# Strassen from the third column pair on, and spatial weights transposed between gate and up, in a two-layer hybrid trunk

## The chip, the cores and the metric

The kernel runs on one core of a Trainium2 chip. The metric is the device time in microseconds from one launch, median over runs. Four engines compute: TensorE (PE, with its weight loads PEld), VectorE (DVE), ScalarE (ACT) and GpSimd (POOL). SyncE (SP) issues transfers (DMAs); an engine's instructions, and a queue's, run in their order.

## The reference

Two layers, 512 tokens, width 1024, all float32. h is the residual stream.

```python
def swiglu(x, w_gu, w_down):
    gate, up = jnp.split(x @ w_gu, 2, axis=-1)
    return (jax.nn.silu(gate) * up) @ w_down

h = h + 0.5 * rmsnorm(swiglu(rmsnorm(h, norm_g[0]), ffn1_gu, ffn1_down), norm_g[1])
z = rmsnorm(h, norm_g[2]) @ w_in      # split into: HGRN2 recurrence, window attention, spatial gating
mixed = jnp.concatenate([o_a, o_b, o_c], axis=-1) @ w_out
h = h + rmsnorm(mixed, norm_g[3])
h = h + 0.5 * rmsnorm(swiglu(rmsnorm(h, norm_g[4]), ffn2_gu, ffn2_down), norm_g[5])
gate = jax.nn.sigmoid(rmsnorm(h, norm_g[6]) @ ple_gate)
h = h + rmsnorm((p_i @ ple_proj) * gate, norm_g[7])
```

The hidden width of the two feed-forward networks (FFN) is 2816, so each has a gate-up matrix of 1024 x 5632 and a down matrix of 2816 x 1024. The spatial gating uses a 128 x 128 lower-triangular matrix per group and layer, sgw; the kernel needs it transposed and masked.

## The kernel before

Every float32 product is made of three products of reduced-precision halves: a value is cast on ScalarE to its high half (L142, L296 and L334, "whi", "uwh") and the difference to the value is the low half, made on VectorE (L139, "wlo", "uwl"). TensorE then adds hi·hi, hi·lo and lo·hi in PSUM.

The phases are ffn1, mix, ffn2 and ple, twice. Each phase ends with a list of chains, one for each of four token tiles: the post-norm of the phase's result, the addition to h (L201) and the pre-norm of the next phase (hn, L225), then transposes on TensorE (ptr, L231) that give hT, the moving operand of the next phase. Of these tile 0 and 1 are transposed at the border, tile 2 and 3 inside the next phase.

An FFN has 11 column pairs, mp = 0 to 10: 256 gate columns and the same 256 up columns. Pair 0 is multiplied plainly, in two halves of the tokens, 192 matmuls of 256 columns (L254). Pairs 1 to 10 use Strassen's scheme on 2 x 2 blocks (halves of the contraction and of the tokens): seven products M1, M2, M5, M6, M3, M7, M4 of 24 matmuls each (L379), with sums of hT blocks made once (token_sums: S1 to S4) and sums of weight blocks made per pair (operands: four raw loads b11, b21, b12, b22 at L329 and five subtractions at L339). Results accumulate in three PSUM banks X, Y, Z. silu(gate)·up goes to a tile g, is stored to DRAM (gd, L416 for pair 0 and L458 for the others) and is loaded again as gl (L484) for the down projection (accs, L249 to L251). M4 of a pair is held back behind M1 of the next pair, except for the last pair.

The order: a scheduler places instructions by their dependences and priorities, except that those passed through pin (keep_in_program_order) keep the order of the program among themselves. Strassen's matmuls are pinned; pair 0's, the raw loads and the g stores are not. issue_after ("behind") puts instructions behind named ones. Weights are staged in two buffers "wst"; buffers "z" and "u" hold raw weights of odd and even pairs. The spatial weights are loaded, transposed (L650) and masked (L652) by mix_params, which a hook calls at k = 4 of the down projection. The stores of h ahead of mix are issued by SP in make_pre.

Of the kernel before, what the change touches and what calls it, by code (L numbers as in the profile page):

```python
# [20 lines left out]
P = 128  # L21
# [51 lines left out]
def kernel(ctx: ExitStack, tc: tile.TileContext, a: dict, out: bass.AP, phases=None):  # L73
# [52 lines left out]
    def tsl(t):  # L126
        return slice(t * P, (t + 1) * P)
# [151 lines left out]
    def ffn(l, w_gu, w_down, i, ends, hook):  # L279
# [4 lines left out]
        def four(x):  # L284
            return x[:].rearrange("p (a b) -> p a b", a=4)
# [5 lines left out]
        for gu in range(2):  # L291
            for q in range(2):
                st = wpool.tile([P, 1024], F32, tag="wst", name="wst", bufs=WST)
                nc.sync.dma_start(four(st), w_view(0, gu, q))
                hi, lo = first[q] if gu == 0 else w_pair()
                nc.scalar.copy(hi[:], st[:])  # L296
                split_lo(lo[:], st[:], hi[:], nc.gpsimd if gu == q == 0 and i == 0 else nc.vector)
                w[gu, q] = hi, lo
        yield
        yield  # L300
        hT = hTs[i]
        turn(0)
        turn(1)

        def token_sums():
            def whole(half, q, tag):
                x = ut("A32", "z") if tag == "z" else wpool.tile([P, 1024], F32, tag=tag, name="A32", bufs=WST)
                hi, lo = (hT[1][y][:, :, HALVES[half]].bitcast(F32) for y in (q, 2 + q))
                pin(nc.vector.tensor_tensor(out=four(x), in0=hi, in1=lo, op=ALU.add))
                return x  # L310

            def make(n, x, y, op, out):
                nc.vector.tensor_tensor(out=out[:], in0=x[:], in1=y[:], op=op)
                nc.scalar.copy(S[n][0][:], out[:])
                split_lo(S[n][1][:], out[:], S[n][0][:])

            a21, a22 = (whole(1, q, "wst") for q in range(2))
            make(1, a21, a22, ALU.add, a22)
            a11 = whole(0, 0, "z")
            make(3, a11, a21, ALU.subtract, a21)  # L320
            make(2, a22, a11, ALU.subtract, a11)
            a12 = whole(0, 1, "z")
            make(4, a12, a11, ALU.subtract, a12)


        def operands(mp):
            def raw(gu, q):
                x = ut("wraw", "z" if mp % 2 else "u")
                nc.sync.dma_start(four(x), w_view(mp, gu, q))  # L329
                return x  # L330

            def split(x):
                hi, lo = w_pair()
                nc.scalar.copy(hi[:], x[:])  # L334
                split_lo(lo[:], x[:], hi[:])
                return hi, lo

            def sub(out, x, y):
                nc.vector.tensor_tensor(out=out[:], in0=x[:], in1=y[:], op=ALU.subtract)  # L339
# [12 lines left out]
            yield split(b22)  # L352
            yield split(b12)
            yield split(b21)
# [14 lines left out]
        def pin(ins):  # L369
            return tc.keep_in_program_order(ins)  # L370
# [9 lines left out]
                                             stop=m == 1 and k == 3 and n == 2, skip_group_check=True))  # L380


        acc = {(m, gu): ps(f"gu{m}{gu}", ("pg", "pm")[m]) for m in range(2) for gu in range(2)}

        def stream():
            for mp in range(1, NMP):
                for (name, kind), w in zip(MS, operands(mp)):
                    yield mp, name, kind, w
        ahead, queue = stream(), []
# [4 lines left out]
                if x:  # L394
                    queue.append(x)

        prefetch(1)
        for tok in HALVES:
            for m in range(2):
                for gu in range(2):  # L400
                    mms = [(k, x) for x in range(3) for k in range(KD)]
                    for k, x in mms:
                        hi, lo = w[gu, k // 4]
                        c = slice((k % 4) * 256 + m * P, (k % 4) * 256 + m * P + P)
                        mm1(acc[m, gu][:, tok], (hi[:, c], lo[:, c]), hT_k(hT, k, tok), x, (k, x) == mms[0], (k, x) == mms[-1])
                    if tok.stop == 256 and 2 * m + gu in FT:
                        turn(2 + FT.index(2 * m + gu))
                if tok.stop == 512:
                    sg = ut("sg", "r")
                    nc.scalar.activation(sg[:], acc[m, 0][:], AF.Silu)  # L410
                    nc.vector.tensor_tensor(out=G[:, m * 512:(m + 1) * 512], in0=acc[m, 1][:], in1=sg[:], op=ALU.mult)
            if tok.stop == 256:
                G = wpool.tile([P, 1024], F32, tag="wst", name="g", bufs=WST)
                token_sums()
                prefetch(2)
        nc.sync.dma_start(gd[0][:], G[:])  # L416


        LOOK = 4
# [8 lines left out]
        def step(mp, name, kind, w):  # L428
# [17 lines left out]
                d["c12"] = ut("c12", "r")  # L446
                nc.scalar.copy(d["c12"][:], X[:])
            if name == "M3":
                d["G"] = wpool.tile([P, 1024], F32, tag="wst", name="g", bufs=WST)
                add(out=d["c12"][:], in0=Z[:], in1=d["c12"][:], op=ALU.add)  # L450
                add(out=g_half(d["G"], 0), in0=m2(d["c12"]), in1=m2(d["c11"]), op=ALU.mult)
            if name == "M7":
                add(out=d["c22"][:], in0=X[:], in1=d["c22"][:], op=ALU.add)  # L453
            if name == "M4":
                sg = ut("sg", "r")
                nc.scalar.activation(sg[:], X[:], AF.Silu)
                add(out=g_half(d["G"], 1), in0=m2(sg), in1=m2(d["c22"]), op=ALU.mult)
                nc.sync.dma_start(gd[mp][:], d["G"][:])  # L458

        held = None  # L460
        while True:
            prefetch(LOOK - len(queue))
            if not queue:
                break
            x = queue.pop(0)
            if x[1] == "M4" and x[0] < NMP - 1:
                held = x
                continue
            step(*x)
            if x[1] == "M1" and held:  # L470
                step(*held)
                held = None

        gpost, npre = ends()
        ORD = {0: "pt", 1: "pg", 2: "pm", 3: "pm"}
        accs = {(t, n): ps(f"acc{t}{n}", ORD[t]) for t in range(NT) for n in range(2)}
        ws, gs = {}, {}
        for k in range(KF):
            if k == 4:
                hook()  # L480
# [6 lines left out]
            gs[k] = tuple(x[:, (k % 2) * 512:(k % 2 + 1) * 512] for x in (gh, gl))  # L487
            if k < KF - TAIL:
                for t in range(NT):
                    for n in range(2):  # L490
                        mm3(accs[t, n][:], cut(gs[k], tsl(t)), ws[k](n * 512), k == 0, False)
# [9 lines left out]
    def ple(l, i, ends):  # L501
# [5 lines left out]
                              a["p"][l, 0, j * 256:(j + 1) * 256, :].rearrange("(t p) c -> p t c", p=P))  # L507
        pT = []
        for k in range(2):
            pt = ps("ppT", "pm")  # L510
# [12 lines left out]
        for t in range(NT):  # L523
# [10 lines left out]
            for u, (n, k) in enumerate(steps):  # L534
# [5 lines left out]
            ys = []  # L540
            for n in range(2):
                y = ut("y", "t")
                nc.scalar.activation(y[:], gt[n][:], AF.Sigmoid)
                out_ = y if t < NT - 1 else pj[n]
                nc.vector.tensor_tensor(out=out_[:], in0=pj[n][:], in1=y[:], op=ALU.mult)
                ys.append(out_[:])
# [3 lines left out]
        chains.append((NT - 1, ys, gpost, 1.0, npre))  # L550
        close_phase()


# [580 lines left out]
    def make_pre(i):  # L1134
# [26 lines left out]
    state = {"setup": not mixers}  # L1161

    def hook_for(i):
        def hook():
            if i + 1 < len(seq) and seq[i + 1][1] == "mix":
                if not state["setup"]:
                    mix_setup()
                    state["setup"] = True
                prms[i + 1] = mix_params(seq[i + 1][0])
        return hook  # L1170

    def phase(i):
# [9 lines left out]
            pass  # L1182

    if seq[0][1] == "mix":
        hook_for(-1)()
    def load_x(t):
        for n in range(2):
            nc.sync.dma_start(h[t][n][:], a["x"][0, tsl(t), HN[n]])
# [8 lines left out]
    next(run)  # L1197
    load_x(2)
    load_x(3)
    pre(2)  # L1200
    pre(3)
    for i in range(len(seq)):
        drain(run)
        todo = list(chains)
# [38 lines left out]
```

## Time and profile before

| what | value |
|---|---|
| median of three runs | 2054.29 us (2050.96, 2054.56, 2054.29) |
| profiled execution | 2056.59 us |
| its span, first to last instruction | 2054.8 us |
| mean granted TensorE clock | 0.985 |
| TensorE busy | 1969.0 us (96%) |
| VectorE, ScalarE busy | 1398.7 us (68%), 925.7 us (45%) |
| GpSimd busy | 113.2 us (6%) |
| instructions | 31098 |

A row of a group gives line, engine, operation, the names out<-in, then busy time and mean duration; a row of waits gives the waiting engine and line, the releaser, and the time in total, the times, and the longest. In rows of windows there follow, behind the window and its length, the busy time (and the count) of PE, PEld, DVE, ACT and POOL, the granted clock, the DMA share and GB/s. Rows of the chain and of the timeline start with the time in us since the first instruction and the duration.

### The profile page before, as it was taken

Reading aid. Unit: us, or ns where it says so; the run is one execution under the profiler, and the core shown is the slowest. Engines: PE = TensorE matmul, PEld = TensorE weight load, DVE = VectorE, ACT = ScalarE, POOL = GpSimd, SP = SyncE. Lnnn points to the kernel's source line nnn. Section 1 sums busy time; section 2 is a strip of 40 time slices with the busy share of each in tenths; the row PEclk is TensorE's granted clock in tenths of the full one; section 3 lists DMA queues with packets and bytes.
Section 4 is the critical chain, followed back from the end, with each engine's and each line's share of the span. In section 5 each row is a group of like instructions: output and inputs, shape, how many; then the busy total and the mean of one; then the engine's idle time right before and its main releaser. Section 6 shows DMA issues by size and latency. Waiting matters only on the chain.

```text
span 2054.8 us, 31098 instructions
## 1 busy us (share of the span) xinstructions
PE 1969.0 (96%) x12524; PEld 1765.8 (86%) x12524; DVE 1398.7 (68%) x2062; ACT 925.7 (45%) x1467; POOL 113.2 (6%) x135
## 2 busy tenths in 40 slices
PE   7899999899999999999989999998999999999998
PEld 6899978688678999888779999786887799998876
DVE  6887753669768888434688886436697688883364
ACT  4445443455444545333445444334555444453252
POOL 1000000112100000000100000001130000000000
PEclk9999999999999999999999999999999999999999
DMA  5434264323404434453234443543232153425431
GB/s 183 142 125 145 72 231 134 103 75 92 130 22 143 153 108 131 143 164 134 82 103 144 126 132 97 197 139 97 62 114 98 42 174 117 141 87 185 159 113 52
DMA packets 160034, 251.18 MB, mean 122 GB/s; under 512 B 11409, under 2 KB 116753, under 8 KB 159889
## 3 DMA queue, kind: packets, MB, share of 16 engines
q1 hardware_dynamic: 159888, 249.19, 37.9%
q8 instruction: 98, 1.61, 0.3%
q14 instruction: 48, 0.39, 0.1%
HBM read 217.17 MB, written 29.36 MB: 120 GB/s over the span
## 4 chain that ended last, share of the span: by engine, by line
PE 66%; DVE 8%; DMA 3%; ACT 2%; issue 1%; POOL 1%; SPq 0%; DVEq 0%; POOLq 0%; ACTq 0%
PE X L379 16%; PE Z L379 9%; PE acc L249 5%; PE acc L251 5%; PE acc L250 5%; PE Y L379 4%; PE gu L254 3%; DMA wraw<-in_ffn_gate_up_dram 1%; PE gate L251 1%; PE gate L249 1%; PE gate L250 1%; DMA wst<-in_ffn_down_dram 1%; PE wo L249 1%; PE ptr L231 1%; PE wo L251 1%
## 5 line engine op out<-in xcount | busy, mean ns | idle before, releaser
L334 ACT CAST whi<-wraw 128x1024 fp32r<-128x1024 f32 x280 | 292.1, 1049 | 371.7 <-DVE wraw L339 147.2
L139 DVE TENSOR_TENSOR wlo<-wraw,whi 128x1024 fp32r<-128x1024 f32 x280 | 340.2, 1222 | 104.8 <-ACT whi L334 102.7
L139 DVE TENSOR_TENSOR wlo<-wst,whi 128x1024 fp32r<-128x1024 f32 x148 | 182.2, 1233 | 169.8 <-ACT whi L142 167.2
L250 PE MATMUL acc<-wlo,gh 128*128 128x512 f32 x704 | 274.8, 390 | 1.0 <-DVE wlo L139 1.0
L249 PE MATMUL acc<-whi,gh 128*128 128x512 f32 x704 | 271.1, 390 | 4.7 <-ACT whi L142 4.7
L251 PE MATMUL acc<-whi,gl 128*128 128x512 f32 x704 | 274.1, 390 | 0.0
L142 ACT CAST whi<-wst 128x1024 fp32r<-128x1024 f32 x140 | 146.8, 1050 | 209.7 <-DMA wst<-in_ffn_down_dram 86.0
L379 PE MATMUL X<-hT,whi 128*128 128x256 f32 x1280 | 232.7, 284 | 3.1 <-DVE c L453 3.1
L339 DVE TENSOR_TENSOR wraw<-wraw 128x1024 f32<-128x1024 f32 x160 | 195.4, 1223 | 12.8 <-DMA wraw<-in_ffn_gate_up_dram 9.0
L379 PEld LDWEIGHTS X<-hT,whi 128*128 128x128 f32 x1280 | 199.7, 192 | 3.9 <-DVE c L453 3.9
L379 PE MATMUL X<-hT,wlo 128*128 128x256 f32 x640 | 181.4, 283 | 0.0
L249 PEld LDWEIGHTS acc<-whi,gh 128*128 128x128 f32 x704 | 131.9, 188 | 33.4 <-ACT whi L142 6.4
L250 PEld LDWEIGHTS acc<-wlo,gh 128*128 128x128 f32 x704 | 132.2, 188 | 29.4 <-DVE wlo L139 2.5
L251 PEld LDWEIGHTS acc<-whi,gl 128*128 128x128 f32 x704 | 132.2, 188 | 28.6 <-DVE gl L486 1.3
L178 POOL TENSOR_TENSOR r<-v,mhalf 128x1 f32<-128x1 f32 x64 | 40.4, 632 | 1746.3 <-DVE v L196 1597.5
L379 PEld LDWEIGHTS X<-hT,wlo 128*128 128x128 f32 x640 | 123.0, 192 | 0.0
L486 DVE TENSOR_TENSOR gl<-gl,gh 128x1024 fp32r<-128x1024 f32 x44 | 53.8, 1223 | 96.5 <-ACT gh L485 96.5
L379 PE MATMUL Y<-hT,whi 128*128 128x256 f32 x640 | 116.9, 284 | 0.0
L379 PE MATMUL Z<-S1h,whi 128*128 128x256 f32 x320 | 95.0, 297 | 12.0 <-ACT whi L334 12.0
L379 PE MATMUL Z<-S1h,wlo 128*128 128x256 f32 x320 | 95.3, 298 | 7.7 <-DVE wlo L139 7.7
L379 PEld LDWEIGHTS Y<-hT,whi 128*128 128x128 f32 x640 | 99.9, 192 | 0.0
L379 PE MATMUL Z<-S1l,whi 128*128 128x256 f32 x320 | 94.4, 295 | 0.0
(324 smaller groups left out, 4635.2 us busy)
## 6 DMA issues: line engine op xcount, KB each, us to landing
wraw<-in_ffn_gate_up_dram SPq DMA_DIRECT2D x160, 512.0 KB, 5.3
wst<-in_ffn_down_dram SPq DMA_DIRECT2D x88, 512.0 KB, 3.3
gd<-g SPq DMA_DIRECT2D x44, 512.0 KB, 6.1
gl<-gd SPq DMA_DIRECT2D x44, 512.0 KB, 3.4
wst<-in_w_in_dram SPq DMA_DIRECT2D x36, 512.0 KB, 3.8
gain<-in_norm_gains_dram SPq DMA_DIRECT2D x32, 256.0 KB, 5.4
wst<-in_ffn_gate_up_dram SPq DMA_DIRECT2D x16, 512.0 KB, 4.5
wst<-in_w_out_dram SPq DMA_DIRECT2D x16, 512.0 KB, 3.4
```

The costliest lines, as they stand in the source:

```text
L139: newest["lo"] = eng.tensor_tensor(out=out_, in0=in_, in1=hi.bitcast(F32), op=ALU.subtract)
L142: newest["hi"] = nc.scalar.copy(out_, in_)
L178: nc.gpsimd.tensor_tensor(out=r, in0=v, in1=mhalf[:, :w], op=ALU.pow)
L231: pin(nc.tensor.transpose(pt[:, j * P:(j + 1) * P], hn[q][:, j * P:(j + 1) * P], ident[:]))
L249: pin(nc.tensor.matmul(acc, lh, rh, start=first, stop=False))
L250: pin(nc.tensor.matmul(acc, lh, rl, start=False, stop=False))
L251: pin(nc.tensor.matmul(acc, ll, rh, start=False, stop=last))
L254: nc.tensor.matmul(acc, lhs[x == 2], rhs[x == 1], start=first, stop=last)
L334: nc.scalar.copy(hi[:], x[:])
L339: nc.vector.tensor_tensor(out=out[:], in0=x[:], in1=y[:], op=ALU.subtract)
L379: pin(nc.tensor.matmul(acc[:, m * 256:(m + 1) * 256], x[:, c], y, start=fresh and m == k == n == 0, stop=m == 1 and k == 3 and n == 2, ski ...
L486: nc.vector.tensor_tensor(out=gl[:], in0=gl[:].bitcast(F32), in1=gh[:].bitcast(F32), op=ALU.subtract)
```

## The change

1. Strassen starts at pair 2. Pair 1 is multiplied plainly as pair 0 is, over all 512 tokens at once: 96 matmuls of 512 columns. Its four weight blocks come through "wst" as well. The plain matmuls (now L408) are pinned: gate and up of the first row half m=0, then of m=1. The sums of tokens all lie in "z", their low halves are split later, and the raw loads (L337) and g stores (L417) are pinned on SP.
2. An FFN's generator yields once more, after the two gate blocks; the last chain of the phase before is put behind their casts.
3. The last M4 is held too: the first down product (tile 0, k = 0) stands ahead of it. g of the last two pairs lies in "z". The gains for the border are loaded after it.
4. mix_params runs at product M2 of pair 5, in Strassen, instead of at k = 4 of the down projection.
5. The stores of h ahead of mix are issued by ScalarE's queue.
6. In ple the last tile's sigmoid and product are built in the chain, the transposes of p use another PSUM bank, and at the program's start tiles 2 and 3 are transposed in the first FFN.

```diff
         for gu in range(2):
             for q in range(2):
...
-                nc.scalar.copy(hi[:], st[:])
+                cast_hi(hi[:], st[:])
...
+                if q and not gu:
+                    yield marks()
         yield
...
             def raw(gu, q):
                 x = ut("wraw", "z" if mp % 2 else "u")
-                nc.sync.dma_start(four(x), w_view(mp, gu, q))
+                pin(nc.sync.dma_start(four(x), w_view(mp, gu, q)))
                 return x
...
         def stream():
-            for mp in range(1, NMP):
+            for mp in range(2, NMP):
...
+        def plain(acc, w, m, gu, tok):
+            mms = [(k, x) for x in range(3) for k in range(KD)]
+            for k, x in mms:
+                hi, lo = w[gu, k // 4]
+                c = slice((k % 4) * 256 + m * P, (k % 4) * 256 + m * P + P)
+                pin(nc.tensor.matmul(acc[m, gu][:, tok], (hi if x < 2 else lo)[:, c], hT_k(hT, k, tok)[x == 1],
+                                     start=(k, x) == mms[0], stop=(k, x) == mms[-1]))
...
+        def store(mp, G):
+            pin(nc.sync.dma_start(gd[mp][:], G[:]))
...
+        acc = plain_banks(0)
+        for m in range(2):
+            for gu in range(2):
+                plain(acc, w, m, gu, HALVES[0])
+                if 2 * m + gu in FT:
+                    turn(2 + FT.index(2 * m + gu))
+        w1 = {}
+        for gu in range(2):
+            for q in range(2):
+                hi, lo = (ut("uwh", "z", F32R), ut("uwl", "z", F32R)) if gu == q == 0 else w_pair()
+                st = wpool.tile([P, 1024], F32, tag="wst", name="wst", bufs=WST)
+                pin(nc.sync.dma_start(four(st), w_view(1, gu, q)))
+                nc.scalar.copy(hi[:], st[:])
+                split_lo(lo[:], st[:], hi[:])
+                w1[gu, q] = hi, lo
+        token_sums()
+        for mp in range(2):
+            G = wpool.tile([P, 1024], F32, tag="wst", name="g", bufs=WST)
+            if mp:
+                acc = plain_banks(1)
             for m in range(2):
                 for gu in range(2):
...
+                    plain(acc, (w, w1)[mp], m, gu, ALL if mp else HALVES[1])
+                plain_out(G, acc, m)
+                if mp:
+                    prefetch(1)
+            store(mp, G)
...
-                d["G"] = wpool.tile([P, 1024], F32, tag="wst", name="g", bufs=WST)
+                d["G"] = ut("g", "z") if mp > NMP - 3 else wpool.tile([P, 1024], F32, tag="wst", name="g", bufs=WST)
...
-            if x[1] == "M4" and x[0] < NMP - 1:
+            if x[:2] == (5, "M2"):
+                hook(0)
+            if x[1] == "M4":
                 held = x
                 continue
...
+                    down(t, k)
+                    if not k and not t:
+                        step(*held)
+                        gpost, npre = ends()
...
         def pre(t, tag="pt", later=False):
+            todo_ = pre_tile(t, g, hTs[i], tag, later)
             for n in range(2):
-                nc.sync.dma_start(away[t][n][:], h[t][n][:])
-            return pre_tile(t, g, hTs[i], tag, later)
+                nc.scalar.dma_start(away[t][n][:], h[t][n][:])
+            return todo_
...
-            with behind(ahead if t == 0 else None):
-                post_tile(t, parts, g, scale)
+            with behind(ahead if t in (0, todo[0][0]) else None):
+                post_tile(t, parts() if callable(parts) else parts, g, scale)
```

TensorE at the head of the first layer's ffn2 (gu_5923 and gu_5925 are gate of m=0 and of m=1, gu_5924 and gu_5926 up of m=0 and m=1; "uwh" is a gate weight, "whi" an up weight). Before:

```order
2996 L254 MATMUL gu_5923<-hT_5190,uwh 128x256 x4
2997 L254 MATMUL gu_5925<-hT_5190,uwh 128x256 x4
2998 L254 MATMUL gu_5923<-hT_5191,uwh 128x256 x4
2999 L254 MATMUL gu_5923<-hT_5192,uwh 128x256 x4
3002 L254 MATMUL gu_5923<-hT_5191,uwl 128x256 x4
3003 L254 MATMUL gu_5925<-hT_5191,uwh 128x256 x4
3007 L254 MATMUL gu_5925<-hT_5191,uwl 128x256 x4
3008 L231 MATMUL ptr<-ident,hn 128x128 x2
3009 L254 MATMUL gu_5924<-hT_5190,whi 128x256 x4
3010 L254 MATMUL gu_5926<-hT_5190,whi 128x256 x4
```

And now, where gu_5828 and gu_5829 are gate and up of m=0, gu_5830 is gate of m=1:

```order
2842 L408 MATMUL gu_5828<-hT_5095,uwh 128x256 x4
2843 L408 MATMUL gu_5828<-hT_5096,uwh 128x256 x4
2844 L408 MATMUL gu_5828<-hT_5097,uwh 128x256 x4
2847 L408 MATMUL gu_5828<-hT_5096,uwl 128x256 x4
2848 L408 MATMUL gu_5829<-hT_5095,whi 128x256 x4
2849 L408 MATMUL gu_5829<-hT_5096,whi 128x256 x4
2852 L408 MATMUL gu_5829<-hT_5095,wlo 128x256 x4
2853 L231 MATMUL ptr<-ident,hn 128x128 x5
2854 L408 MATMUL gu_5829<-hT_5096,wlo 128x256 x4
2855 L408 MATMUL gu_5830<-hT_5095,uwh 128x256 x4
```

Before, the gate products of both row halves stood ahead of the first up product; now 24 of them do, and up of m=0 comes ahead of gate of m=1.

SP in the same FFN, ahead of the first Strassen pair. Before (wraw_6308, 6310, 6343 and 6374 belong to pair 2, wraw_5927, 5929, 6066 and 6072 to pair 1):

```order
177 L294 DMA wst_5876<-in_ffn2_gate_up_dram 128x4x256
178 L294 DMA wst_5882<-in_ffn2_gate_up_dram 128x4x256
179 L329 DMA wraw_6308<-in_ffn2_gate_up_dram 128x4x256
180 L329 DMA wraw_6310<-in_ffn2_gate_up_dram 128x4x256
181 L329 DMA wraw_6343<-in_ffn2_gate_up_dram 128x4x256
182 L329 DMA wraw_6374<-in_ffn2_gate_up_dram 128x4x256
183 L329 DMA wraw_6066<-in_ffn2_gate_up_dram 128x4x256
184 L416 DMA gd0_5912<-g_6045 128x1024
185 L329 DMA wraw_6072<-in_ffn2_gate_up_dram 128x4x256
```

Now (wraw_6146, 6148, 6205 and 6212 are b11, b21, b12 and b22 of pair 2):

```order
172 L433 DMA wst_5962<-in_ffn2_gate_up_dram 128x4x256
173 L417 DMA gd0_5817<-g_5986 128x1024
174 L337 DMA wraw_6146<-in_ffn2_gate_up_dram 128x4x256
175 L337 DMA wraw_6148<-in_ffn2_gate_up_dram 128x4x256
176 L337 DMA wraw_6205<-in_ffn2_gate_up_dram 128x4x256
177 L417 DMA gd1_5818<-g_6090 128x1024
178 L337 DMA wraw_6212<-in_ffn2_gate_up_dram 128x4x256
179 L337 DMA wraw_6345<-in_ffn2_gate_up_dram 128x4x256
```

Three of the raw loads of the first Strassen pair stand behind the store of pair 0's g, and the fourth behind the store of pair 1's.

VectorE around the masking of the transposed spatial weights. Before, at the end of ffn1 in the first layer:

```order
220 L197 SCALAR_TENSOR_TENSOR tmp<-acc_2766,gain_2746 128x512
221 L196 TENSOR_SCALAR v<-ssq 128x1
222 L197 SCALAR_TENSOR_TENSOR tmp<-acc_2767,gain_2748 128x512
223 L201 SCALAR_TENSOR_TENSOR h<-tmp,r,h 128x512
224 L652 TENSOR_TENSOR wT<-wT,triu 128x512
225 L201 SCALAR_TENSOR_TENSOR h<-tmp,r,h 128x512
227 L222 TENSOR_SCALAR v<-ss 128x1
228 L225 SCALAR_TENSOR_TENSOR hn<-h,r,gain_2750 128x512
```

Now it stands between operands of Strassen pairs:

```order
85 L489 TENSOR_TENSOR g<-sg,c_1177 128x2x256
86 L139 TENSOR_TENSOR wlo<-wraw,whi 128x1024
87 L700 TENSOR_TENSOR wT<-wT,triu 128x512
88 L472 TENSOR_TENSOR c_1390<-Y,c_1390 128x512
89 L139 TENSOR_TENSOR wlo<-wraw,whi 128x1024 x2
```

The masking stood inside the post-norm of tile 0; it now stands inside the gate-up part.

More of the change, by code (lines that the diff above doesn't have):

```diff
@@ L305, in token_sums, with whole @@
         def token_sums():
-            def whole(half, q, tag):
-                x = ut("A32", "z") if tag == "z" else wpool.tile([P, 1024], F32, tag=tag, name="A32", bufs=WST)
+            def whole(half, q):
+                x = ut("A32", "z")
                 hi, lo = (hT[1][y][:, :, HALVES[half]].bitcast(F32) for y in (q, 2 + q))
-                pin(nc.vector.tensor_tensor(out=four(x), in0=hi, in1=lo, op=ALU.add))
+                nc.vector.tensor_tensor(out=four(x), in0=hi, in1=lo, op=ALU.add)
                 return x
@@ L314, in make, with low @@
                 nc.scalar.copy(S[n][0][:], out[:])
[L315 to L317 removed]
+            def low(n, x):
+                split_lo(S[n][1][:], x[:], S[n][0][:])
+            a21, a22 = whole(1, 0), whole(1, 1)
             make(1, a21, a22, ALU.add, a22)
[L319 removed]
+            a11 = whole(0, 0)
+            low(1, a22)
             make(3, a11, a21, ALU.subtract, a21)
             make(2, a22, a11, ALU.subtract, a11)
[L322 removed]
+            low(2, a11)
+            low(3, a21)
+            a12 = whole(0, 1)
             make(4, a12, a11, ALU.subtract, a12)
+            low(4, a12)
         def operands(mp):
@@ new lines, in plain_out, with plain_banks @@
+        def plain_out(G, acc, m):
+            sg = ut("sg", "r")
+            nc.scalar.activation(sg[:], acc[m, 0][:], AF.Silu)
+            nc.vector.tensor_tensor(out=G[:, m * 512:(m + 1) * 512], in0=acc[m, 1][:], in1=sg[:], op=ALU.mult)
+        def store(mp, G):
+            pin(nc.sync.dma_start(gd[mp][:], G[:]))
+        def plain_banks(mp):
+            return {(m, gu): ps(f"gu{m}{gu}", (("pg", "pt")[mp], "pm")[m]) for m in range(2) for gu in range(2)}
+        acc = plain_banks(0)
[4 more added lines that the diff above has]
+                    turn(2 + FT.index(2 * m + gu))
@@ L472, in ffn, with down @@
                 held = None
-        gpost, npre = ends()
         ORD = {0: "pt", 1: "pg", 2: "pm", 3: "pm"}
-        accs = {(t, n): ps(f"acc{t}{n}", ORD[t]) for t in range(NT) for n in range(2)}
+        accs = {}
         ws, gs = {}, {}
+        def down(t, k):
+            for n in range(2):
+                if not k:
+                    accs[t, n] = ps(f"acc{t}{n}", ORD[t])
+                mm3(accs[t, n][:], cut(gs[k], tsl(t)), ws[k](n * 512), k == 0, False, pin if not k else lambda x: x)
         for k in range(KF):
             if k == 4:
-                hook()
+                hook(1)
             ws[k] = load_w(w_down[k * P:(k + 1) * P, :])
```

61 lines of the change are left out of this document (23 added, 38 removed).

## The prediction

> **What bounds the kernel now.** I read the page's head first, then the waits of TensorE, then stretches of the clock, and last the chain inside those stretches.
>
> ```profile
> span 2054.8 us, 31098 instructions
> PE 1969.0 (96%) x12524; PEld 1765.8 (86%) x12524; DVE 1398.7 (68%) x2062; ACT 925.7 (45%) x1467; POOL 113.2 (6%) x135
> ```
>
> TensorE sets the end: 1969 of 2054.8 us. A change can only add or remove matmul time, idle time on TensorE, or time at a lower clock. The waits of TensorE that the change touches (engine, line, releaser: us in total, times, longest):
>
> ```profile
> PE ptr L231 <- DVE hn L225: 26.7, 14, 8.3
> PE Z L379 <- ACT whi L334: 12.0, 4, 3.8
> PE Z L379 <- DVE wlo L139: 7.7, 4, 4.2
> PE acc L249 <- ACT whi L142: 4.7, 4, 1.4
> PE gu L254 <- ACT uwh L296: 3.4, 4, 1.6
> PE X L379 <- DVE c L453: 3.1, 4, 0.8
> PE acc L250 <- DVE wlo L139: 1.0, 1, 1.0
> ```
>
> The two Z rows come four times each, once per FFN: M5 of the first Strassen pair. The chain of waits around the second FFN says why: a raw weight was issued only at 637.20, its landing took 8.70 us, and its subtractions follow on VectorE.
>
> ```profile
> 637.20 8.70 DMA wraw<-in_ffn_gate_up_dram
> 645.92 1.23 DVE wraw L339
> 648.88 1.14 DVE wlo L139
> 650.07 5.06 PE Z L379 x22
> ```
>
> The 22 matmuls take 0.23 us each there instead of 0.12, because the clock was down. Each of the four stalls is followed by such a stretch (columns: length, busy us of PE, PEld, DVE, ACT, POOL, then PEclk):
>
> ```profile
> 54.70:61.50 6.80, 4.43 (x20) 4.43 (x21) 6.73 (x6) 2.94 (x3) 0.00 (x0) 0.50 0.04 13
> 648.60:655.50 6.90, 5.64 (x27) 5.43 (x26) 6.87 (x7) 3.76 (x5) 0.00 (x0) 0.51 0.24 76
> 1075.30:1082.10 6.80, 6.19 (x29) 6.19 (x30) 6.77 (x7) 3.98 (x6) 0.00 (x0) 0.50 0.29 82
> 1662.40:1669.20 6.80, 5.43 (x23) 5.13 (x24) 6.77 (x8) 3.28 (x5) 0.00 (x0) 0.50 0.25 78
> ```
>
> **What the change removes.** *First Strassen pair.* It now comes one pair later, with 33 us or more between the token sums and the first M5 (half of the plain pair 0, 11.5 us, and all of pair 1, 21.8 us), so the S operands and the first raw weights are there. The waits of 12.0 + 7.7 = 19.7 us go. Busy time at half clock was 4.43 + 5.64 + 6.19 + 5.43 = 21.7 us; half of it, 10.8, was loss. Together −30.5.
>
> *End of Strassen.* The last M4 waited for c of L453 (3.1 us in all), and the second down product for its weight (4.7 + 1.0). Now six 512-column products (6 x 0.227, row below) stand ahead of that M4, and the last two g lie in "z", which frees the weight buffer earlier. −8.8; bounds −3 (if the weight stays late, 5.7 remain) and −8.8.
>
> *FFN1 to mix.* VectorE sat 14.4 us in front of the masking of the transposed spatial weights, with the post-norm queued behind it, and TensorE then waited for that norm and ran at half clock:
>
> ```profile
> DVE wT L652 <- PE wT L650: 28.8, 2, 14.4
> 383.30 1.11 PE L231 MATMUL ptr<-ident,hn 128*128 128x128 f32 x4 [4.27 <-DVE hn L225]
> 382.40:389.20 6.80, 5.90 (x18) 4.70 (x19) 6.71 (x12) 5.37 (x15) 0.66 (x3) 0.50 0.45 151
> 1399.60:1406.40 6.80, 4.68 (x15) 3.78 (x16) 6.07 (x12) 5.18 (x13) 1.10 (x2) 0.50 0.45 152
> ```
>
> The transposes move into Strassen of pair 4 and 5, where VectorE has 3.8 us free per pair (the 20.16-us row below: 16.35 busy). The other layer's stall is alike: 2 x 4.27 = 8.5, and half of 5.90 + 4.68 = 5.3, together 13.8. What is late next is the hn of the following tile; I keep 2 us for it: −12, bounds −5 and −13.8. The h stores go to ScalarE's queue, eight per layer; eight issues at SP's 0.37 each are 3 us of an engine that is 45% busy: nothing, or up to 1 us if a cast of hT stands behind one.
>
> **What it adds.** *Pair 1 plain.* One Strassen pair takes 20.16 us, all busy; 18 matmuls of 512 columns take 4.08 us, so 0.227 each, and 96 of them 21.8.
>
> ```profile
> 687.42:707.58 20.16, 20.16 (x170) 20.16 (x169) 16.35 (x17) 9.82 (x13) 0.00 (x0) 1.00 0.43 132
> 609.78 0.23 PE wo L251
> 613.86 0.24 PE wo L251
> ```
>
> So +1.6 per FFN, +6.5 in four.
>
> *Head of an FFN.* Before, gate of both row halves (m=0 and m=1) ran while the up weights came. Now the order is pinned: gate m=0, up m=0. In the second FFN before:
>
> ```profile
> 613.92 1.12 PE L254 MATMUL gu<-hT,uwh 128*128 128x256 f32 x8
> 615.79 1.70 PE L254 MATMUL gu<-hT,uwh 128*128 128x256 f32 x12 [0.76 <-ACT uwh L296]
> 615.05 2.34 SPq L294 DMA_DIRECT2D wst<-in_ffn_gate_up_dram  x2
> 618.99 1.03 ACT L296 CAST whi<-wst 128x1024 fp32r<-128x1024 f32 x1
> 620.91 1.06 ACT L296 CAST whi<-wst 128x1024 fp32r<-128x1024 f32 x1 [0.90 <-DMA wst<-in_ffn_gate_up_dram]
> 621.06 1.19 PE L254 MATMUL gu<-hT,whi 128*128 128x256 f32 x8
> 639.26 0.40 PE L379 MATMUL X<-hT,whi 128*128 128x256 f32 x2
> ```
>
> The 24 gate matmuls (2.9 us) end near 617.0. The first up cast ends at 620.0, so TensorE waits 3.0; four matmuls on, at 620.6, it waits for the second cast until 621.1 to 622.0, some 1.2. The gate gap of 0.76 goes, since both gate casts now precede the post-norm. Tiles 2 and 3 are transposed later in turn, behind the casts for pair 1, estimated at 1.7. Net 3.0 + 1.2 − 0.8 + 1.7 = 5.1, and one clock window (below) of 1.7: +7 each, +14 in the two FFN2. Lower bound: 0, if the post-norm standing behind the casts brings the up weights earlier. FFN1 had waits of its own there; I put +4 on both together (0 to 8).
>
> *M6 of pair 2.* SP's queue is pinned: the store of pair 1's g (L417) now stands ahead of the fourth raw weight, b22, and waits for the last plain product. No trace shows it; the nearest rows:
>
> ```profile
> wst<-in_ffn_down_dram SPq DMA_DIRECT2D x88, 512.0 KB, 3.3
> wraw<-in_ffn_gate_up_dram SPq DMA_DIRECT2D x160, 512.0 KB, 5.3
> wst<-in_ffn_gate_up_dram SPq DMA_DIRECT2D x16, 512.0 KB, 4.5
> L339 DVE TENSOR_TENSOR wraw<-wraw 128x1024 f32<-128x1024 f32 x160 | 195.4, 1223 | 12.8 <-DMA wraw<-in_ffn_gate_up_dram 9.0
> ```
>
> From the end T of pair 1 on TensorE: g 0.7, store issue 0.4, so b22 is issued at T + 1.2. It lands 3.3, 4.5 or 5.3 us later; three subtractions and the low split (4 x 1.22) put M6's operand at T + 9.4, 10.6 or 11.4. M1, M2 and M5 take 3 x 2.88 (20.16 in seven), and the third matmul of M6 needs it at T + 8.9: a stall of 0.5, 1.7 or 2.5. The store is in flight beside it, so the middle: 1.7 x 4 = 7, and 1 us for the clock: +8 (2 to 17). Behind it on SP wait the raw weights of pair 3; they have the four products from M6 on, 11.5 us.
>
> *Clock after short gaps.* Two like gaps of 2.4 us, at the start of ffn2 in both layers:
>
> ```profile
> 601.10:604.30 3.20, 0.92 (x6) 0.43 (x5) 1.68 (x4) 0.84 (x4) 0.55 (x1) 0.99 0.02 7
> 604.30:607.70 3.40, 3.40 (x12) 2.83 (x11) 1.42 (x3) 1.17 (x2) 0.00 (x0) 0.51 0.00 0
> 1616.80:1619.90 3.10, 0.83 (x6) 0.42 (x4) 1.58 (x4) 0.81 (x4) 0.55 (x1) 1.00 0.00 0
> 1619.90:1623.30 3.40, 3.40 (x19) 2.76 (x18) 1.39 (x3) 1.17 (x2) 0.00 (x0) 1.00 0.00 0
> ```
>
> One lost the clock for 3.4 us (1.7 us of work), one did not. I charge 1.7 for a head with two gaps, little for M6. The Trainium skill, TensorE: Matmul & The Clock Gate, section "HAM oscillation — how this bites in real kernels", gives the rule that gaps of up to about 3.4 us keep the clock. The window at 604.30 speaks against it, that at 1619.90 for it; by the rule the clock terms of the new waits would be nothing.
>
> *The rest* I put at nothing: the sigmoid of ple's last tile and the gains, issued later, and the PSUM banks of "ppT" and "wT", all of it work off TensorE. Without cover it is one tile's chain, an activation and a product of 0.6 to 0.7 us in two layers, under 3 us.
>
> **Sum.** −30.5 − 8.8 − 12 + 6.5 + 14 + 4 + 8 = −18.8, against the profiled execution's 2056.6 (span 2054.8): 2037.8. The median of the runs, 2054.3, is 2.3 below it: 2035.
>
> **Rivals.** *A, the waits do not appear* (0.17): up weights and b22 are in time, so 14 + 4 + 8 fall away: 2009 to 2013. For it: the same buffers and queue deliver 512 KB in 3.3 us when alone. Against it: in the rows above SP issued the up weights only at 615.05.
>
> *B, b22 becomes the bound* (0.13), on the slower side. The load behind the store lands as late as the one at 637.20, 8.7 us after issue: the operand is at T + 14.8, the stall 5.9, and as after every stall above 4 us here the clock halves for 6.8 us, another 3.4: 9.3 x 4 = 37 instead of 8, hence 2064. It decides from 6.8 us per FFN (19 more in four), that is a landing beyond 6.2 us. For it: a loss of that kind stands in the Z rows. Against it: then five loads were in flight, here one store.
>
> *C, FFN1 to mix stays bound by the norm chain* (0.14): TensorE still waits some 4.3 us, and the clock falls: 12 are not gained, 2047.
>
> *D, no clock loss after short gaps* (0.10): two heads' 1.7, the like in FFN1 and M6's 1 fall away, some 6 us: 2029. The page of the Trainium skill named above states this rule.
>
> **How the numbers follow.** My forecast, 2035, has 0.46; its own range is 2024 to 2046 from the bounds above. A is left out in part below 2014, B above 2053: range 2014 to 2053. A measurement here can tell about 0.2%, 4 us. Faster by more: the forecast, A, D and most of C, 0.82. Within: the rest of C and an edge of the forecast, 0.06. Slower: B, 0.12.
>
> **What would show it.** Right: no Z wait at the first M5 and no half clock there; no VectorE wait at wT; the row of M4's X and of the second down product gone; new waits of "gu" on whi at four heads and of "X" on wlo in pair 2. Wrong: waits at M6 above 4 us with half clock (B), heads without waits (A), or "ptr" still waiting 4 us at FFN1 to mix (C).

## The result, and the profile after

The changed kernel takes 2082.61 us (median of 4 runs, 2080.16 to 2087.27) against 2052.79 us before (4 runs): ratio 1.0148, interval 1.0126 to 1.0170. It is slower by 29.8 us where 19 faster was forecast, and it lies outside the range of 2014 to 2053. One execution of a later run, the one with SP freed and the spatial weights loaded earlier, took 6805.49 us and is left out of its median. The head of the page after:

```profile
span 2081.6 us, 30397 instructions
PE 1985.8 (95%) x12236; PEld 1765.3 (85%) x12236; DVE 1345.7 (65%) x2022; ACT 904.5 (43%) x1443; POOL 113.3 (5%) x135
```

The span is 26.8 us longer. VectorE and ScalarE do less than before, TensorE is busy 16.8 us more, and the rest is waiting. Those waits of TensorE after that bear on the change (engine, line, releaser: us in total, times, longest):

```profile
PE ptr L231 <- DVE hn L225: 25.2, 11, 8.0
PE gu L408 <- ACT whi L142: 11.6, 7, 4.3
PE acc L249 <- ACT gh L525: 10.8, 4, 3.7
PE X L387 <- DVE wlo L139: 6.9, 4, 1.8
PE X L387 <- DVE c L485: 5.5, 9, 1.2
PE gate L249 <- DVE tmp L197: 3.0, 2, 1.7
PE acc L251 <- DVE gl L526: 2.3, 4, 0.7
PE X L387 <- ACT whi L342: 1.3, 3, 0.5
```

The Z rows of M5 are gone. In their place stand four things: up weights at the head ("gu"), the reload of g at the first down product ("gh", "gl"), M6's operand ("X" on wlo and whi), and c of L485, now at the borders of pairs too. The ptr row lost the two stalls at mix, yet is hardly smaller: a new one came at ple.

Cut at the first matmul of each stage on TensorE's timeline, the two profiled executions differ as follows (my sums; "excess" is what exceeds the products, 2.88 us for one of Strassen's and 0.227 us for a plain matmul of 512 columns; pair 1 plain stands at those sizes, and what exceeds them is in the row below it):

| stage, all its occurrences | forecast, us | measured, us |
|---|---|---|
| pair 1 plain, 4 x 1.6 | +6.5 | +6.5 |
| plain part, head waits and clock | +18 | +18.6 |
| first M5, waits and clock | −30.5 | −31.5 |
| rest of Strassen: M6 and borders of pairs, excess | +8 | +21.9 |
| end of Strassen and down projection | −8.8 | +12.0 |
| border to mix, and mix | −12 | −12.1 |
| border to ple, and ple | 0 | +10.8 |
| start | 0 | +0.4 |
| sum | −18.8 | +26.6 |

The terms of pair 1, the plain part, the first M5 and mix came out within 2 us. Three did not (the rest of Strassen, its end, and ple), and they are the 45 us by which the sum was off.

**The end of Strassen.** The chain of waits after, in ffn2 of the first layer (start, us, what):

```profile
845.44 1.51 PE X L387 x13
850.99 4.32 DMA gl<-gd
855.33 1.05 ACT gh L525
856.41 1.24 DVE gl L526
857.69 0.51 PE acc L251
859.25 4.01 PE X L387 x24
```

TensorE's first down product waits for g of pair 0, whose reload was issued only at 850.99. On SP's timeline before and after, in the same stage:

```profile
810.53 0.34 SPq L484 DMA_DIRECT2D gl<-gd  x1
817.32 0.32 SPq L484 DMA_DIRECT2D gl<-gd  x1
```

```profile
847.74 3.20 SPq L160 DMA_DIRECT2D wst<-in_ffn_down_dram  x2
850.99 0.42 SPq L524 DMA_DIRECT2D gl<-gd  x1
```

Before, the two reloads were out 39 and 32 us ahead of the first down product (849.14). Now g of the last two pairs takes their "z" buffers, and the reload stands on SP behind down weights that wait for theirs. Since the product also moved ahead of M4, M4 stands behind it, and its matmuls run at half clock (24 in 4.01 us, not 2.88).

**The border to ple.** ScalarE's timeline after, then TensorE's, then ScalarE's before:

```profile
982.48 0.58 ACT L243 CAST pTh<-ppT 128x512 fp32r<-128x512 f32 x1 [9.23 <-PE ppT L554]
982.96 0.63 ACT L220 ACTIVATE hn<-h 128x512 f32<-128x512 f32 x1
986.17 0.63 PE L231 MATMUL ptr<-ident,hn 128*128 128x128 f32 x4 [3.29 <-DVE hn L225]
```

```profile
962.31 0.63 ACT L220 ACTIVATE hn<-h 128x512 f32<-128x512 f32 x1
```

ScalarE sat idle for 9.23 us in front of the cast of p's transposes, which waited for TensorE to finish the down projection, with the squares of the pre-norm (hn, L220) behind it. Before, those squares ran at 962.31, 8.5 us ahead of the border. It is the mechanism that the masking of the spatial weights had on VectorE before, now on ScalarE.

**The clock.** Windows after (length, busy us, and PEclk behind POOL's):

```profile
987.90:994.90 7.00, 5.29 (x14) 4.10 (x13) 6.84 (x11) 4.64 (x12) 0.55 (x1) 0.51 0.26 82
858.30:861.70 3.40, 3.40 (x16) 3.21 (x15) 1.23 (x1) 1.04 (x1) 0.00 (x0) 0.51 0.76 276
257.60:264.40 6.80, 5.47 (x18) 4.38 (x19) 4.21 (x18) 2.78 (x7) 0.00 (x0) 0.50 0.72 271
680.00:683.40 3.40, 1.63 (x11) 1.43 (x12) 3.40 (x4) 3.40 (x5) 0.00 (x0) 1.00 0.64 205
```

These stretches lie at the new stalls: at ple (987.90), at the end of Strassen in the second FFN and the first (858.30 and 257.60), and at M6 of the second FFN (680.00). The stalls at the end and at ple cost clock as well; this one at M6 does not.

**SP's queue.** Around the ninth pair after, and the median landings:

```profile
822.14 0.34 SPq L417 DMA_DIRECT2D gd<-g  x1
822.57 2.65 SPq L337 DMA_DIRECT2D wraw<-in_ffn_gate_up_dram  x4
```

```profile
wraw<-in_ffn_gate_up_dram SPq DMA_DIRECT2D x144, 512.0 KB, 6.2
gd<-g SPq DMA_DIRECT2D x44, 512.0 KB, 3.1
```

A store of g waits for its pair's last product; the four raw loads pinned behind it are then issued in one burst, and land 6.2 us after issue instead of 5.3.

### The profile page after: what moved, and what is told of

Its sections match the earlier page's. It is cut to its first block, busy times and chain, and to the rows that moved or that the text cites. A ratio compares the mean times of both kernels' runs of the same rounds, so it can differ in the third digit from the quotient of the medians.

```text
span 2081.6 us, 30397 instructions
## 1 busy us (share of the span) xinstructions
PE 1985.8 (95%) x12236; PEld 1765.3 (85%) x12236; DVE 1345.7 (65%) x2022; ACT 904.5 (43%) x1443; POOL 113.3 (5%) x135
## 4 chain that ended last, share of the span: by engine, by line
PE 64%; DVE 16%; DMA 9%; ACT 5%; issue 4%; POOL 1%; SPq 1%; DVEq 0%; POOLq 0%; ACTq 0%
PE X L387 10%; PE acc L251 8%; PE acc L249 7%; PE acc L250 7%; PE gu L408 7%; DMA wraw<-in_ffn_gate_up_dram 6%; PE Z L387 4%; DVE wlo L139 3%; DVE wraw L347 3%; PE Y L387 3%; DMA wst<-in_ffn_gate_up_dram 2%; ACT whi L342 2%; PE gate L249 1%; PE gate L250 1%; PE gate L251 1%
## 5 line engine op out<-in xcount | busy, mean ns | idle before, releaser
L342 ACT CAST whi<-wraw 128x1024 fp32r<-128x1024 f32 x252 | 258.0, 1050 | 348.1 <-DVE wraw L347 237.6
L139 DVE TENSOR_TENSOR wlo<-wraw,whi 128x1024 fp32r<-128x1024 f32 x252 | 302.7, 1221 | 146.3 <-ACT whi L342 135.8
L139 DVE TENSOR_TENSOR wlo<-wst,whi 128x1024 fp32r<-128x1024 f32 x160 | 196.3, 1229 | 171.1 <-ACT whi L142 163.5
L249 PE MATMUL acc<-whi,gh 128*128 128x512 f32 x704 | 275.1, 391 | 10.8 <-ACT gh L525 10.8
L387 PE MATMUL X<-hT,whi 128*128 128x256 f32 x1152 | 216.1, 289 | 5.7 <-DVE c L485 5.5
L347 DVE TENSOR_TENSOR wraw<-wraw 128x1024 f32<-128x1024 f32 x144 | 174.9, 1221 | 29.2 <-DMA wraw<-in_ffn_gate_up_dram 27.2
L387 PEld LDWEIGHTS X<-hT,whi 128*128 128x128 f32 x1152 | 184.4, 196 | 9.6 <-DVE c L485 8.2
L249 PEld LDWEIGHTS acc<-whi,gh 128*128 128x128 f32 x704 | 132.4, 188 | 39.8 <-ACT gh L525 11.6
L387 PE MATMUL X<-hT,wlo 128*128 128x256 f32 x576 | 165.1, 287 | 0.0
L525 ACT CAST gh<-gl 128x1024 fp32r<-128x1024 f32 x44 | 46.3, 1052 | 145.8 <-PE acc L250 127.5
L408 PE MATMUL gu<-hT,whi 128*128 128x256 f32 (+1 forms) x448 | 85.5, 340 | 11.6 <-ACT whi L142 11.6
L387 PE MATMUL X<-S2h,wlo 128*128 128x256 f32 x288 | 82.6, 287 | 6.9 <-DVE wlo L139 6.9
```

What stands on the lines that cost most here:

```text
L139: newest["lo"] = eng.tensor_tensor(out=out_, in0=in_, in1=hi.bitcast(F32), op=ALU.subtract)
L249: pin(nc.tensor.matmul(acc, lh, rh, start=first, stop=False))
L387: pin(nc.tensor.matmul(acc[:, m * 256:(m + 1) * 256], x[:, c], y, start=fresh and m == k == n == 0, stop=m == 1 and k == 3 and n == 2, ski ...
L408: pin(nc.tensor.matmul(acc[m, gu][:, tok], (hi if x < 2 else lo)[:, c], hT_k(hT, k, tok)[x == 1], start=(k, x) == mms[0], stop=(k, x) == m ...
L525: nc.scalar.copy(gh[:], gl[:].bitcast(F32))
```

## The experiments

Differences are medians against the runs of the kernel before in the same call; the change itself stands at +29.8 us.

### One undo at a time, from the changed kernel

```diff
-            pt = ps("ppT", "pt")
+            pt = ps("ppT", "pm")
```

> Undoes one line: the transposes of p in ple go to the PSUM bank they had before ("pm" instead of "pt"). Theory 1: in the changed kernel the cast of these transposes stands on ScalarE ahead of the pre-norm's squares and waits for TensorE until the tail of the down projection is over, so that TensorE then waits 3.5 us and more for hn and runs at half clock; ple took 72.7 and 76.0 us instead of 67.7 and 70.1. With the old bank the cast comes later, both come back: 2082.6 - 10.8 = 2072. Rival: the norm is late because it stands behind the casts of the next phase's weights: no change, 2081 to 2084.

2068.56 us, ratio 1.0069 (1.0050 to 1.0088): +14.4, so this one word costs 15 us; theory 1 had 10.8. The waits of its profile:

```profile
PE ptr L231 <- DVE hn L225: 17.5, 10, 7.7
```

The stalls of some 3.3 us at ple have left the row. On ScalarE the squares now stand 8.7 us ahead of the border to ple (TensorE's transposes of hn at 974.91), with no cast of p's transposes before them:

```profile
966.20 0.63 ACT L220 ACTIVATE hn<-h 128x512 f32<-128x512 f32 x1
```

The rival (casts of the next phase ahead of the norm) falls.

```diff
-                pin(nc.sync.dma_start(four(x), w_view(mp, gu, q)))
+                nc.sync.dma_start(four(x), w_view(mp, gu, q))
...
-            pin(nc.sync.dma_start(gd[mp][:], G[:]))
+            nc.sync.dma_start(gd[mp][:], G[:])
```

> Undoes two lines: raw loads and g stores are no longer pinned on SP. Theory 1: the pinned queue holds the fourth raw weight behind the store of pair 1's g (M6 of pair 2 waits 6.9 + 1.3 us in all, and once the clock falls, 1.7) and later issues the four raw loads of a pair in a burst behind each g store, so that VectorE is late and the X bank waits for c of L485 (5.5): these go, some 15 us in all, 2067. Rival: the loads are late because of the traffic itself, not of their place: the same waits, 2080 to 2084. Against both: freed, the scheduler may put a load of a later pair ahead, and a wait like that of the first M5 before comes back.

2079.07 us, ratio 1.0115 (1.0087 to 1.0144): +24.9, only 5 us gained. The waits at M6 and c are gone, but a new one stands in the profile, up to 5.7 us in each layer, each with 6.8 us at half clock:

```profile
PE wT L698 <- DMA sgw<-in_sg_spatial_w_dram: 11.3, 2, 5.7
```

Unpinned, raw loads of later pairs stand ahead of the spatial weights on SP and wait for buffers. The run alone did not tell the theories apart; the next group does.

```diff
-                d["G"] = ut("g", "z") if mp > NMP - 3 else wpool.tile(...)
+                d["G"] = wpool.tile(...)
...
-            if x[1] == "M4":
+            if x[1] == "M4" and x[0] < NMP - 1:
...
-                    if not k and not t:
-                        step(*held)
-                        gpost, npre = ends()
```

> Undoes the end of Strassen: the last M4 is not held, no down product stands ahead of it, the gains are loaded ahead of the down projection, and g of the last two pairs lies in the weight staging buffers again. Theory 1: the product ahead of M4 waits for gh (10.8 us in four, 2.3 for gl, and the clock falls four times, 8.5), because g in "z" takes the buffers in which the first reload of g came 40 us ahead: 21.5 us go, and the waits of before (8.8) come back, 2070. Rival: the reload is late because the pinned queue of SP holds it behind the down weights: the wait moves to the first down product behind M4, 2078 to 2083.

2069.16 us, ratio 1.0073 (1.0048 to 1.0098): +15.0, 15 us gained. Only the first of these edits:

> The changed kernel with one line undone: g of the last two pairs lies in the weight staging buffers, not in "z"; the down product stays ahead of the last M4. Theory 1: the first reload of g is early again and the wait for gh (10.8 us and four stretches of low clock) goes, all or more of what undoing the whole end gave: 2082.6 - 14 to 18, 2065 to 2069. Rival (the order is the cost): the wait at the product stays, 2078 to 2084.

2068.65 us, ratio 1.0067 (1.0045 to 1.0089): +14.8. The one line gives as much as undoing the whole end, so the place of g is the cost, not the order of product and M4. In its profile SP issues the first reload at 799.88 in the same FFN, 49 us ahead of the product:

```profile
799.88 16.58 SPq L524 DMA_DIRECT2D gl<-gd  x2
```

The product ahead of M4 now waits for its weight's low half instead of g:

```profile
PE acc L250 <- DVE wlo L139: 7.7, 5, 1.7
```

```diff
-                pin(nc.tensor.matmul(acc[m, gu][:, tok], ...
+                (pin if tok is ALL else lambda i: i)(nc.tensor.matmul(acc[m, gu][:, tok], ...
```

> Undoes the pinned order of pair 0's plain products (pair 1 stays pinned). Theory 1: with the scheduler free to put gate of m=1 ahead of up of m=0, the head's waits for the up weights ("gu" on whi, 11.6 us in all, with two stretches of 6.8 us at half clock) fall away in both ffn2: 2082.6 - 13 = 2069. Rival: the up weights are late themselves, because the casts ahead of the norm hold ScalarE, and the order does not matter: 2079 to 2083.

2058.28 us, ratio 1.0024 (1.0009 to 1.0039): +4.2. With 25.6 us this is the largest gain of the four; expected were 13. The up weights' wait is down from 11.6:

```profile
PE gu L408 <- ACT whi L142: 2.3, 5, 0.7
```

In the profiled execution the plain parts are 16.6 us shorter; it was one of the slowest of ten (2065.14, in 2053.12 to 2065.91), so the other 9 us of the median's gain are not located. The up weights were not late, the order asked for them too early.

```diff
-                nc.scalar.dma_start(away[t][n][:], h[t][n][:])
+                nc.sync.dma_start(away[t][n][:], h[t][n][:])
```

> The changed kernel with one edit undone: SP issues the stores of h, as before, still behind the pre-norm in the program. Theory 1: they are off the path on either queue, 2080 to 2085. Rival (on ScalarE's queue they spare SP a wait ahead of mix's weights): slower by 3 or more, 2086 and above.

2078.64 us, ratio 1.0116 (1.0072 to 1.0161): +24.8. Its interval overlaps that of the change; whether the queue of the h stores matters by some us stays open. The rival, that ScalarE's queue helps by 3 or more, has the sign against it, but the edge of the interval still reaches it.

### Together, and SP's queue by itself

The edits of the bank for p's transposes, of the whole end of Strassen and of pair 0's order, all three as shown above, in one kernel:

> The three undos together: old PSUM bank for the transposes of p, the end of Strassen as before, pair 0's plain products not pinned. The queue of SP stays pinned. Theory 1 (separate waits on TensorE, which add): 2082.6 - 14.0 - 13.4 - 24.3 = 2031, 22 below before; left are the waits at M6 and at c. Rival (the waits are one slack that moves on: what is gained in one stage is lost in the next): clearly less, 2045 or more.

2040.56 us, ratio 0.9923 (0.9909 to 0.9938): −15.9. From +29.8, the three single gains (15.4 + 14.8 + 25.6) would give −26.0; 10 are missing. The result lies between theory 1 (22 below before) and the rival (8 or less below). But the changed kernel's time enters this comparison twice, with an interval of 4.5 us to each side, so 10 is no more than these medians can leave open. In the profiled executions the spans shrink by 14.9, 8.5 and 18.2 us one at a time, 41.6 in sum, and by 43.0 together. That the waits do not add is thus not shown. Left in its profile:

```profile
PE X L387 <- DVE wlo L139: 6.6, 4, 1.8
PE X L387 <- DVE c L485: 5.9, 8, 1.4
PE acc L249 <- ACT whi L142: 5.8, 4, 1.8
```

To these three is added:

```diff
-            pin(nc.sync.dma_start(gd[mp][:], G[:]))
+            pin(nc.gpsimd.dma_start(gd[mp][:], G[:]))
```

> As the three undos together, and the g stores are issued by GpSimd's queue, so that no raw load stands behind a store on SP; the raw loads stay pinned. Theory 1 (place in the queue): the waits at M6 of pair 2 (some 9 us with the clock) and at c (5) go, 2031 - 12 = 2019. Rival (the four loads are late because a burst of four shares the engines, or b22 waits for its buffer): unchanged, 2029 to 2033.

2017.51 us, ratio 0.9811 (0.9796 to 0.9826): −38.9, 23 us below the three undos. This is the fastest kernel of the study. Of the waits on X nothing is left but c ahead of the last M4:

```profile
PE X L387 <- DVE c L485: 3.1, 4, 0.8
```

Strassen's excess is down from some 22 us to some 4, while traffic and loads are the same. The raw loads land 5.2 us after issue (median), not 6.2, and a store takes longer to land than with the three undos alone (3.2 us; page, DMA issues):

```profile
gd<-g POOLq DMA_DIRECT2D x44, 512.0 KB, 5.6
```

So it was the place in SP's queue, not the traffic. The Trainium skill, DMA: Bandwidth & Descriptors, section "Issuing engines are not separate DMA queues", says that issuing from several engines saves only the time on the sequencer, usually small. Here it saved 23 us, because what the store held on SP was not an issue of 0.34 us but its wait for a product.

Instead of that, the three undos with the two pins of SP undone as above, and the spatial weights loaded earlier and apart from their transposes:

```diff
+            if x[:2] == (4, "M5"):
+                hook(0)        # loads of the spatial weights
+            if x[:2] == (5, "M6"):
+                hook(2)        # their transposes and mask
```

> As the three undos together, raw loads and g stores not pinned, and the spatial weights loaded at M5 of pair 4 and transposed at M6 of pair 5. With SP free, M6 and c had no wait left, but TensorE waited 11.3 us for the spatial weights' load, which then stood behind raw loads that wait for buffers, and ran at half clock after it. Theory 1: loaded one pair earlier, that wait goes: 2031 - 15 = 2016. Rival: the small load is late wherever it stands among raw loads: 2028 to 2032.

2022.72 us (median of three), ratio 0.9831 (0.9812 to 0.9851): −33.7, 18 below the three undos, near theory 1 (15). The waits for the spatial weights, at M6 and at the borders of pairs are gone from its profile. With the small load one pair earlier, freeing SP gains what the second run did not show.

### Parts of the change by themselves

The same two hooks, in the kernel before, in place of the one at k = 4 of the down projection:

> The kernel before, and of the change only the move of the spatial weights: loaded at M5 of pair 4, transposed and masked at M6 of pair 5. Theory 1: the block of 14.4 us on VectorE at the border to mix, the wait of 4.3 us and the half clock go, in two layers: 2053.5 - 12 = 2041 to 2042. Rival (the norm's chain is bound by something else as well): 2049 or more.

2040.83 us, ratio 0.9927 (0.9912 to 0.9942): −15.6, where 12 were expected. Against the rows before, only the ptr row of its profile is clearly smaller (26.7 before), and Z is as before:

```profile
PE ptr L231 <- DVE hn L225: 19.1, 13, 7.9
PE Z L379 <- ACT whi L334: 11.7, 4, 3.7
```

The move of the spatial weights alone beats the kernel before.

Then, from the fastest kernel:

```diff
-            for mp in range(2, NMP):
+            for mp in range(1, NMP):
...
-        for mp in range(2):
+        for mp in range(1):
             G = wpool.tile([P, 1024], F32, tag="wst", name="g", bufs=WST)
```

> As the kernel with the three undos and the g stores on GpSimd's queue (2017.5), but Strassen starts at the second pair again: only pair 0 is plain, the token sums and the first M5 lie one after the other. Theory 1: the four stalls at the first M5 come back (19.7 us of waits and 10.8 us of half clock), and the plain pairs' 6.5 us go: 2017.5 + 24 = 2041. Rival (the stall came from raw loads held up on SP, as the 8.7-us landing suggested, and GpSimd's queue for the stores frees them): the stall is half or less, so that the plain pair gains little, 2011 to 2026.

2028.77 us, ratio 0.9875 (0.9859 to 0.9891): −25.1, so the plain second pair is worth 13.8 us here, not 24. The rival is nearer. The first M5 and M6 wait like this:

```profile
PE Z L387 <- DVE wlo L139: 5.3, 4, 1.3
PE X L387 <- DVE wlo L139: 3.0, 4, 0.8
PE X L387 <- ACT whi L342: 2.0, 4, 0.5
```

M5 waits 5.3 us instead of 19.7, M6 another 5, and the clock falls after none of them. So much of the stall that the change went round is gone without it. Raw loads in order and no g store ahead of them are the likely reason; the sums of tokens are built otherwise than before as well, and no run separates the two.

And from the fastest kernel, the order of the change at the end of Strassen again:

```diff
-            if x[1] == "M4" and x[0] < NMP - 1:
+            if x[1] == "M4":
...
+                    if not k and not t:
+                        step(*held)
+                        gpost, npre = ends()
```

> As the kernel with the three undos and the g stores on GpSimd's queue, and the end of Strassen as the change has it (last M4 held, the first down product ahead of it, the gains after it), but with g of the last pairs in the weight staging buffers, so that "z" stays free and the first reload of g comes early. Theory 1 (the reload was late, not the product too early): no wait for gh, and the 0.94 us before each last M4 go too: 2017.5 - 4 = 2013 to 2014. Rival (the product ahead of M4 takes weights and casts when VectorE and ScalarE have no time for them): TensorE waits there for whi or wlo, 2017 to 2027.

2021.42 us, ratio 0.9842 (0.9824 to 0.9861): −32.4, no gain over −38.9, and rather slower. The 0.8 us at M4 went, and 1.7 came at the product ahead of it in each FFN, as the rival had it:

```profile
PE acc L250 <- DVE wlo L139: 7.2, 5, 1.7
```

## Why the prediction was wrong

**First M5, pair 1 plain, heads, mix: right in sum, the heads partly by luck.** The four terms were −30.5, +6.5, +18 and −12, and measured −31.5, +6.5, +18.6 and −12.1. The reading from the waits' rows with half of the busy time at half clock held. The head's +18, worked out from when the casts of the up weights ended, was in the row for "gu" (11.6) and two stretches of clock (half of 6.23 and of 6.42 us), and freeing the order gave it back. But the parts were off against each other: in each ffn2 new waits of 3.0 + 1.2 + 1.7 were forecast and 4.6 and 3.7 came, with a clock loss of 3.1 and 3.2 instead of 1.7. One thing behind the M5 term was incomplete: it did not ask what a plain pair is worth if the loads come in order. The run that starts at the second pair shows M5 with 5.3 us of waits and no half clock, so the plain pair was not the only way round that stall.

**The end of Strassen, −8.8, was the step that failed most.** It argued that "the last two g lie in "z", which frees the weight buffer earlier". It asked what the edit frees and not what it takes: "z" held the early reload of g, and the new first product needs exactly that. Measured +12.0, 21 us off. The one-line run shows it (g in the weight buffers, 15 us gained). The bounds, −3 and −8.8, had no loss in them, though no row excluded one.

**"The rest I put at nothing": ple, +10.8 in the profile and 15 us by its run.** The bank of "ppT" was called work off TensorE with less than 3 us at stake. But with the other bank the scheduler put the cast earlier in ScalarE's queue, where it waits for TensorE, ahead of the squares; with the old bank it stands behind them. That the bank is free earlier is my reading of why, and no run shows it. The prediction had just taken 13.8 us for that very pattern at mix.

**M6 and the pinned queue, +8, was right in mechanism and too small.** M6's stall was put at 1.7 each and measured 1.6 to 2.3; with the half clock after one of the four that is some 10 us. But I ended the argument at the first pair: "Behind it on SP wait the raw weights of pair 3; they have the four products from M6 on". The pinned store holds the raw loads of every later pair as well, and the borders of pairs add as much again. The excess was 21.9 us; with the three undos, moving the stores to GpSimd took all but 4 of it.

**The clock.** Charging 1.7 for heads with two gaps was too little there (6.8 us at half clock in both ffn2, with gaps of 4.3 and 3.3 us on TensorE; the two gaps that the prediction calls 2.4 are 3.20 less 0.92 and 3.10 less 0.83, so 2.3). At the end of Strassen gaps of 2.2 to 2.5 us were followed by 3.4 us at half clock in all three FFNs that had them; at M6 a gap of 1.8 us was in one FFN of the four. The gap alone does not settle it: in the profile with the old bank for "ppT" half clock follows M6's gaps in three FFNs of four, and in that with the three undos in none. The rule of the Trainium skill in TensorE: Matmul & The Clock Gate, section "HAM oscillation — how this bites in real kernels", that gaps up to some 3.4 us keep the clock, does not hold for these, and rival D with it.

**Rivals.** B named the slower side and the queue, but not the price: M6 never came near 5.9 us. A and C did not happen.

What stays open: whether the three undos add up, 9 us of the gain from pair 0's order that its profile does not show, how much of the first M5's stall was the order on SP, and a possible few us of the h stores' queue.

## What to carry to other kernels

When an edit moves a buffer or a bank, list what had it before and what will be placed earlier because of it, on the in-order engines too: an instruction that waits for TensorE and stands ahead of a norm cost some 15 us twice over here, on VectorE before the change and, cured there, on ScalarE after it. A store that waits for a result does not belong in the queue that issues the next operands; moved to a little-used engine's queue it gave 23 us. And an order pinned for one stage has to be followed through the later stages that it also pins.

## What was not expected of the hardware

Nothing in a new kind of behaviour, but one size, the median landing of the 512-KB stores of g. From SP with the loads pinned behind them it was 3.1 to 3.2 us in seven kernels, from SP without that pin 5.8 to 6.3 in four (6.1 before), and from GpSimd, with the loads free of them, 5.6 to 5.7 in three. So in these runs the longer landing goes with free loads, not with the engine that issues the store. Each issue held GpSimd for 0.53 us, an engine 5% busy in the changed kernel and 7% with the stores:

```profile
L417 POOL DMA_DIRECT2D gd<-g x44: 531/531/727, 45.0 to 1829.2; - x44
```
